# Attention scores as pairs of 64-row products, and the low parts of weight units on another engine

## The chip, the cores and the metric

The kernel runs on one core of one Trainium2 chip. The metric is the device time of one execution in microseconds, the median of several runs. The core has five engines that work from queues of their own: TensorE (PE; its weight loads are shown apart as PEld), VectorE (DVE), ScalarE (ACT), GpSimd (POOL), and SyncE (SP), which issues most of the transfers. Products are accumulated in PSUM; everything else lies in SBUF, both with 128 partitions.

## The reference

A small transformer of two layers works on 512 latent tokens with 256 context tokens ahead of them, 1024 features each. Layer 0 mixes the tokens with a bidirectional mLSTM, layer 1 with windowed attention; a squared-ReLU network follows each. The change lies in layer 1's attention alone:

```python
SWA_HEADS, SWA_KV_HEADS, SWA_DH = 16, 4, 64    # four query heads share one key head
# for each block j of 128 latent queries (four of them), each key head, its four query heads:
s_lat = where(valid, einsum("bqhgd,bkhd->bhgqk", qb, kb) * scale, -inf)  # blocks j-1, j, j+1
s_ctx = einsum("bqhgd,bchd->bhgqc", qb, ck) * scale                      # all 256 context tokens
m = max(max(s_lat), max(s_ctx), sink)
p = exp(s - m);  den = sum(p) + exp(sink - m)
o = (p_lat @ vb + p_ctx @ cv) / den
```

A key is valid for a query when they are at most 128 positions apart. The products must be more exact than one pass with the numbers' high parts, so each number is split: a high part that TensorE takes as it is, and a low part, the rest. A product of two split numbers is then high by high, high by low and low by high (low by low is small).

## The kernel before

The attention is worked in 16 tiles (g, j): key head g from 0 to 3, query block j from 0 to 3. The scores of a tile have 128 rows of queries for each of four heads, and W columns: the two or three neighbouring blocks of keys and 256 of context. W is 512 for j of 0 and 3, and 640 for j of 1 and 2.

**Queries and keys.** `q_out` (line 1888) turns the projected queries of one tile, splits them, and lays high and low part of a head side by side, 64 and 64 columns; a transpose puts them below one another, so that a head has 128 partitions: 64 of high part and 64 of low part. `kv_out` (line 1860) makes two copies of the keys in the same way: in k0 the high part lies above the low one, in k1 the low one above the high one. One 128-row product of a head with k0 gives high by high plus low by low, one with k1 gives the two mixed terms.

**Scores.** `scores` (line 1905) goes through the four heads one after the other. Each has two products for the 256 columns of context (lines 1927 and 1928) and two for the latent columns (1929 and 1934). Between the latter lie one or two products of a bf16 identity with a bf16 mask (1931, 1933) which add -1e30 where a key is out of the window: one for j of 0 and 3, two else. The result `s` is a PSUM tile of 1024 columns, which spans two banks; the pool `sc` has two buffers of it. A tile of 512 columns a head takes two heads into one buffer, one of 640 columns one head. When a buffer is full, VectorE takes the maximum (1940) and makes the negative bias nb (1942), and ScalarE makes the exponentials e with their sums (1947). For two heads at a time VectorE then makes the reciprocal of the denominator and GpSimd scales e (1958).

**Values.** `weigh` (line 1962) transposes the weights of a tile, 128 columns of all four heads at a time (1974), ScalarE takes the high part ph (1979) and VectorE the low part pl (1980), and two products with the values follow (1989, 1990).

**Order.** Everything is written as generators, and a pattern, `PAT` in line 18, says how the steps of a tile are interleaved: S is the next step of the scores of the tiles ahead, T a turn of weights, V a pair of value products, F a step of filler, that is of a projection of keys, values or queries for later tiles (six products of 256 columns) or of the output projection of the previous key head (three of 512 columns). Scores have four steps for each tile, one a head, and run somewhat more than a tile ahead. A scheduler then lays out each engine's instructions by readiness and priority; `keep_in_program_order` holds a single instruction behind its predecessor on the engine. On the chip each engine takes its instructions strictly in the order laid out.

**Weight units.** `unit` (line 73) loads 128 x 1024 weights by SyncE into `raw` (three buffers) and calls `split` (line 1034): ScalarE copies the high part `whi`, and the engine handed in, else VectorE, subtracts to get the low part `wlo` (line 1038). During the attention the units of the query projection (wsq, two for each key head) and of the output projection (wsout, two for each) come this way.

Layer 0 has 64-row products of its own, which the change doesn't touch: lines 931 and 988 take two heads of 64 features alternately, one in the upper and one in the lower 64 partitions, each into a PSUM bank of its own.

Of the kernel before, what the change touches and what calls it, by code (L numbers as in the profile page):

```python
# [9 lines left out]
F32 = mybir.dt.float32  # L10
F32R = mybir.dt.float32r
BF16 = mybir.dt.bfloat16
AF = mybir.ActivationFunctionType
ALU = mybir.AluOpType
# [7 lines left out]
P = 128  # L22
D = 1024
KT = D // P
NL = 512
NCX = 256
T = NL + NCX
# [7 lines left out]
DH = 64  # L35
# [21 lines left out]
class Trunk:  # L57
    def __init__(self, tc, ctx, aps):
        self.tc, self.nc, self.ctx, self.a = tc, tc.nc, ctx, aps
        self.nq = 0  # L60
        self.ada_todo = []
        self.ada_every = 0
        self.ada_cap = None
        self.pin = self.pin_mm = False
        self.ada_due = 0.0


# [966 lines left out]
    def split(self, src, hi, lo, eng=None):  # L1034

        keep = self.tc.keep_in_program_order if self.pin else lambda i: i
        keep(self.nc.scalar.copy(out=hi, in_=src))  # L1037
        keep((eng or self.nc.vector).tensor_tensor(out=lo, in0=src, in1=hi.bitcast(F32), op=ALU.subtract))  # L1038

    def feed(self, pin=False):  # L1040

# [590 lines left out]
    def layer1_mix(self, u):  # L1632
        nc, tc, a = self.nc, self.tc, self.a
        self.ctx_ada.close()
        with tc.tile_pool(name="sw", bufs=1, reuse_waits="tile") as sw:
# [8 lines left out]
            idb = sw.tile([P, P], BF16, name="idb")  # L1644
            nc.gpsimd.tensor_copy(out=idb, in_=self.ident)
            msk = []
# [37 lines left out]
            with tc.tile_pool(name="sc", bufs=2, space=PSUM, reuse_waits="tile") as sc, \  # L1684
# [33 lines left out]
                def filler(n):  # L1718
# [7 lines left out]
                        yield  # L1726
                    yield from its

                curs = [[] for _ in todo]

                def all_scores():
# [11 lines left out]
                for n, (g, j) in enumerate(todo):  # L1743
                    if ys[g] is None:
                        ys[g] = sw.tile([P, 2, NL], F32, name=f"yT{g}", tag="yT", bufs=2)
                    if j == 0 and g:
                        parts = self.out_part(g - 1, ys, pt, "pt")
                    if n == 14:
                        y3 = self.split_y(3)
                        st3 = {"y": y3}  # L1750
                        self.st = {}
                        self.tmpA = [self.base.tile([P, NL], F32, name=f"nA{t}", tag=t) for t in ("uH5", "uL5", "uL4")]
                        pa = self.out_part(3, ys, pt, "pt", "A", st3)
                        parts = [f for i in range(4) for f in (parts[i], pa[i])] + pa[4:5]
                        self.split_half(ys[3], y3, 0)
                    fl = filler(n)
                    wg = self.weigh(sw, g, j, curs[n], pt, av, ys)
                    for cmd in PAT if n < 15 else PL:
                        next({"S": sg, "F": fl}.get(cmd) or wg[cmd], None)
                    for it in (wg["T"], wg["V"], fl):  # L1760
                        for _ in it:
                            pass
# [97 lines left out]
    def kv_out(self, sw, pr, j, ps, eng):  # L1860

        nc = self.nc
        d = self.swd
        vt, v = d["vst"][j, pr], ps[:, 128:256].rearrange("p (h d) -> p h d", d=DH)
        nc.scalar.copy(out=vt[:, :, 0, :], in_=v)
        nc.vector.tensor_tensor(out=vt[:, :, 1, :], in0=v, in1=vt[:, :, 0, :].bitcast(F32), op=ALU.subtract)
        if j < 4:
            k = self.rope(sw, j, ps[:, 0:128], 2, eng)
        else:
            k = sw.tile([P, 640], F32, name="rp1", tag="e", bufs=12)[:, :128].rearrange("p (h d) -> p h d", d=DH)  # L1870
            nc.scalar.copy(out=k, in_=ps[:, 0:128].rearrange("p (h d) -> p h d", d=DH))

        sp = sw.tile([P, 2, 4, DH], F32R, name="ksp", tag="sp", bufs=4)
        kk = k.unsqueeze(2).broadcast_to([P, 2, 2, DH])
        nc.scalar.copy(out=sp[:, :, 0::3, :], in_=kk)
        nc.vector.tensor_tensor(out=sp[:, :, 1:3, :], in0=kk, in1=sp[:, :, 0::3, :].bitcast(F32), op=ALU.subtract)

        def late():
            pt = self.ptp.tile([P, 512], F32R, name="pt", tag=self.ptag)
            for i in range(2):  # L1880
                for h in range(2):
                    nc.tensor.transpose(out=pt[:, (2 * i + h) * P:(2 * i + h + 1) * P],
                                        in_=sp[:, h, 2 * i:2 * i + 2].rearrange("p a d -> p (a d)"), identity=self.identr)
            nc.any.tensor_copy(out=d["ks"][pr][:, :, :, j * P:(j + 1) * P],
                               in_=pt.rearrange("p (i h t) -> p i h t", i=2, h=2))
        return late

    def q_out(self, sw, g, j, ps, eng):
        nc = self.nc
        qs = self.swd["qs"]  # L1890
        q = self.rope(sw, j, ps, 4, eng)
        sp = sw.tile([P, 4, 2, DH], F32R, name="qsp", tag="sp", bufs=4)
        nc.scalar.copy(out=sp[:, :, 0, :], in_=q)
        nc.vector.tensor_tensor(out=sp[:, :, 1, :], in0=q, in1=sp[:, :, 0, :].bitcast(F32), op=ALU.subtract)

        def late():
            pt = self.ptp.tile([P, 512], F32R, name="pt", tag=self.ptag)
            for i in range(4):
                nc.tensor.transpose(out=pt[:, i * P:(i + 1) * P],
                                    in_=sp[:, i].rearrange("p a d -> p (a d)"), identity=self.identr)  # L1900
            qs[g, j] = sw.tile([P, 4, P], F32R, name="qs", tag="qs", bufs=5)
            nc.any.tensor_copy(out=qs[g, j], in_=pt.rearrange("p (h t) -> p h t", t=P))
        return late

    def scores(self, sw, g, j, scp, out):

        nc = self.nc
# [8 lines left out]
        nb = sw.tile([P, 4], F32, name="nb", tag="nb", bufs=2)  # L1916
        es = sw.tile([P, 4], F32, name="es", tag="es", bufs=2)
        per = 2 if W == 512 else 1
        views = []
        for i in range(4):  # L1920
            if i % per == 0:
                s = scp.tile([P, 1024], F32, name="s", tag="s")
                views = []
            ql = q4[:, i, :]
            c0 = (i % per) * 512 if per == 2 else 512 - wl
            lat, cx = s[:, c0:c0 + wl], s[:, c0 + wl:c0 + W]
            mm(out=cx, lhsT=ql, rhs=k0[:, NL:T], start=True, stop=False)
            mm(out=cx, lhsT=ql, rhs=k1[:, NL:T], start=False, stop=True)
            mm(out=lat, lhsT=ql, rhs=k0[:, lo * P:hi * P], start=True, stop=False)
            if j > 0:  # L1930
                mm(out=lat[:, 0:P], lhsT=d["idb"], rhs=d["msk"][0], start=False, stop=False)
            if j < 3:
                mm(out=lat[:, wl - P:wl], lhsT=d["idb"], rhs=d["msk"][1], start=False, stop=False)
            mm(out=lat, lhsT=ql, rhs=k1[:, lo * P:hi * P], start=False, stop=True)
            views.append(s[:, c0:c0 + W])
            if i % per == per - 1:
                i0 = i + 1 - per
                mx = sw.tile([P, 2], F32, name="mx", tag="mx", bufs=4)[:, 0:per]
                keep = self.tc.keep_in_program_order if g + j == 0 else lambda x: x
                keep(nc.vector.reduce_max(out=mx, in_=s.rearrange("p (h w) -> p h w", h=2) if per == 2 else views[0],  # L1940
                                          axis=AX.X))
                keep(nc.vector.scalar_tensor_tensor(
                    out=nb[:, i0:i0 + per], in0=mx, scalar=-(DH ** -0.5),
                    in1=d["nsink"][:, g * 4 + i0:g * 4 + i0 + per], op0=ALU.mult, op1=ALU.min))
                for ii, sv in zip(range(i0, i0 + per), views):
                    e = sw.tile([P, 640], F32, name="e", tag="e", bufs=12)
                    nc.scalar.activation(out=e[:, :W], in_=sv, func=AF.Exp, scale=DH ** -0.5, bias=nb[:, ii:ii + 1],
                                         accum_out=den[:, ii:ii + 1])
                    out.append(e)
            if i % 2:  # L1950
                pr = slice(i - 1, i + 1)
                nc.vector.tensor_tensor(out=es[:, pr], in0=nb[:, pr],
                                        in1=self.sink[:, g * 4 + i - 1:g * 4 + i + 1], op=ALU.add)
                nc.scalar.activation(out=es[:, pr], in_=es[:, pr], func=AF.Exp)
                nc.vector.tensor_tensor(out=den[:, pr], in0=den[:, pr], in1=es[:, pr], op=ALU.add)
                nc.vector.reciprocal(out=den[:, pr], in_=den[:, pr])  # L1956
                for ii in (i - 1, i):
                    nc.gpsimd.tensor_scalar(out=out[ii][:, :W], in0=out[ii][:, :W], scalar1=den[:, ii:ii + 1],  # L1958
                                            scalar2=1.0, op0=ALU.mult, op1=ALU.mult)
            yield  # L1960

    def weigh(self, sw, g, j, ps_, ptp, avp, ys):
# [194 lines left out]
```

## Time and profile before

| | |
|---|---|
| runs (three) | 1531.76, 1531.79, 1532.83 us, median 1531.79 |
| profiled execution | 1531.83 us |
| its span, first to last instruction | 1530.0 us |
| granted TensorE clock, mean | 0.997 |
| attention stage | about 955 to 1200 us of the span |
| score products (lines 1927 to 1934) | 352 matmuls, 955.8 to 1157.1 us |

In the profile's rows a line number stands for a line of the kernel, `out<-in` names tiles, and a shape such as 64*128 in a matmul's row gives the rows and columns of the array that it uses, followed by the shape that streams through. A group's row gives the time that the group kept its engine busy, the mean length of one instruction in ns, and, behind the second bar, how long the engine was idle ahead of them and what ended it. A row of a window gives its limits, its length, and for PE, PEld, DVE, ACT and POOL the busy time with the number of instructions, then the granted clock, the share of the transfers, and GB/s; asked for one tile, it leaves out engines that don't touch it. A row of the waits says who waited for whom, for how long in sum, how often, and the longest wait. Matmuls run in a pipeline: the length of one reaches beyond the start of the next.

### The profile page before, as it was taken

What the parts mean: (1) busy time and instruction counts of PE and PEld (TensorE: products, weight loads), DVE (VectorE), ACT (ScalarE), POOL (GpSimd) and SP (SyncE); (2) the same over time, 40 slices, a digit from 0 to 9 for tenths busy, and PEclk for the clock granted to TensorE, in tenths of its full rate; (3) what the DMA queues carried; (4) which work ended last, traced back from release to release, by engine and by line L of the source; (5) the groups of instructions that cost most, each with busy time, mean ns of one, the idle gap of its engine ahead of it and who ended that gap; (6) DMA issues with size and microseconds to landing.
All of it is one profiled execution on the core that took longest, in us unless ns stands there. A gap on an engine that the chain in (4) does not pass through costs nothing.

```text
span 1530.0 us, 23829 instructions
## 1 busy us (share of the span) xinstructions
PE 1505.8 (98%) x9129; PEld 1349.1 (88%) x9129; DVE 1135.0 (74%) x2074; ACT 739.8 (48%) x1494; POOL 310.7 (20%) x312
## 2 busy tenths in 40 slices
PE   9999999999999999999999999999999999999998
PEld 5888888878889999999999999888887988888886
DVE  4985638497797768777776668788888875757697
ACT  4544242443674352423515355575666665445454
POOL 0112021311203222322333230343443000000000
PEclk9999999999999999999999999999999999999999
DMA  9133313244132334244343422010101524140321
GB/s 378 70 102 120 111 56 121 66 148 148 56 97 69 124 125 151 97 152 131 131 152 103 145 73 73 29 42 28 56 31 39 182 94 138 55 152 28 110 70 55
DMA packets 46632, 157.27 MB, mean 103 GB/s; under 512 B 5135, under 2 KB 7695, under 8 KB 46391
## 3 DMA queue, kind: packets, MB, share of 16 engines
q1 hardware_dynamic: 45344, 154.25, 30.4%
q8 instruction: 72, 1.18, 0.3%
q10 hardware_dynamic: 1175, 1.51, 0.3%
q14 instruction: 41, 0.34, 0.1%
HBM read 153.64 MB, written 2.10 MB: 102 GB/s over the span
## 4 chain that ended last, share of the span: by engine, by line
PE 79%; DVE 7%; ACT 5%; issue 4%; POOL 3%; DMA 1%; POOLq 0%; DVEq 0%; ACTq 0%
PE mm L102 50%; PE p L102 7%; PE pj L102 4%; PE kept L102 3%; PE pt L1974 1%; PE acc L102 1%; PE pc L102 1%; PE at L993 1%; DVE adap L269 1%; ACT whi L1037 1%; DVE wlo L1038 1%; PE pb L102 1%; PE av L1989 1%; PE av L1990 1%; PE at L956 1%
## 5 line engine op out<-in xcount | busy, mean ns | idle before, releaser
L102 PE MATMUL mm<-h,whi 128*128 128x384 f32 x1024 | 264.1, 338 | 1.4 <-ACT h L1037 0.8
L1038 DVE TENSOR_TENSOR wlo<-raw,whi 128x1024 fp32r<-128x1024 f32 (+2 forms) x152 | 178.2, 1176 | 81.1 <-ACT whi L1037 78.9
L1037 ACT CAST whi<-raw 128x1024 fp32r<-128x1024 f32 (+2 forms) x152 | 150.8, 998 | 144.3 <-PE mm L102 96.1
L102 PE MATMUL mm<-uH,whi 128*128 128x512 f32 (+1 forms) x496 | 189.5, 386 | 0.0
L102 PEld LDWEIGHTS mm<-h,whi 128*128 128x128 f32 x1024 | 185.5, 188 | 4.1 <-ACT h L1037 1.9
L102 PE MATMUL mm<-uL,whi 128*128 128x512 f32 (+1 forms) x496 | 186.5, 378 | 0.8 <-DVE uL L339 0.4
L102 PE MATMUL mm<-uH,wlo 128*128 128x512 f32 (+1 forms) x496 | 186.9, 378 | 0.0
L269 DVE SCALAR_TENSOR_TENSOR adap<-raw,crow 128x1024 bf16<-128x1024 f32 x128 | 161.6, 1262 | 21.4 <-DMA raw<-ada 20.6
L102 PE MATMUL mm<-h,wlo 128*128 128x384 f32 x512 | 172.1, 336 | 0.0
L102 PE MATMUL p<-t,whi 128*128 128x384 f32 x448 | 114.2, 336 | 0.0
L1037 ACT CAST whi<-sum 128x512 fp32r<-128x512 f32 (+1 forms) x42 | 31.8, 760 | 159.8 <-PE mm L102 59.8
L102 PEld LDWEIGHTS mm<-uH,wlo 128*128 128x128 f32 x496 | 93.3, 188 | 17.8 <-issue 0.9
L102 PEld LDWEIGHTS mm<-uL,whi 128*128 128x128 f32 x496 | 93.6, 189 | 16.7 <-DVE uL L651 0.7
L102 PEld LDWEIGHTS mm<-uH,whi 128*128 128x128 f32 x496 | 92.9, 189 | 15.6 <-issue 0.3
L102 PEld LDWEIGHTS mm<-h,wlo 128*128 128x128 f32 x512 | 96.1, 188 | 0.0
L1038 DVE TENSOR_TENSOR wlo<-wb,whi 128x1024 fp32r<-128x1024 f32 x49 | 59.1, 1221 | 36.5 <-ACT whi L1037 36.3
L1038 DVE TENSOR_TENSOR h<-r,h 128x384 fp32r<-128x384 f32 (+2 forms) x100 | 58.5, 587 | 32.9 <-ACT h L1037 32.6
L102 PEld LDWEIGHTS p<-t,whi 128*128 128x128 f32 x448 | 81.3, 188 | 0.0
L102 PE MATMUL mm<-uC,whi 128*128 128x256 f32 x416 | 79.5, 290 | 0.3 <-ACT whi L1037 0.3
L1037 ACT CAST whi<-wb 128x1024 fp32r<-128x1024 f32 x49 | 51.5, 1054 | 57.5 <-PE mm L102 47.8
L102 PE MATMUL p<-t,wlo 128*128 128x384 f32 x224 | 75.3, 336 | 0.0
L1958 POOL TENSOR_SCALAR e<-e,den 128x512 f32<-128x512 f32 (+1 forms) x64 | 49.2, 783 | 126.9 <-DVE den L1956 80.2
(411 smaller groups left out, 3787.9 us busy)
## 6 DMA issues: line engine op xcount, KB each, us to landing
raw<-ada SPq DMA_DIRECT2D x80, 512.0 KB, 3.6
raw<-w SPq DMA_DIRECT2D x64, 512.0 KB, 3.5
raw<-w2a SPq DMA_DIRECT2D x32, 512.0 KB, 3.5
wb<-w2b SPq DMA_DIRECT2D x28, 512.0 KB, 4.1
adaw<-ada SPq DMA_DIRECT2D x16, 512.0 KB, 11.2
raw<-wqk SPq DMA_DIRECT2D x8, 512.0 KB, 4.0
raw<-wv SPq DMA_DIRECT2D x8, 512.0 KB, 3.5
raw<-wo SPq DMA_DIRECT2D x8, 512.0 KB, 3.5
```

Source lines behind the costliest of these rows:

```text
L102: i = self.nc.tensor.matmul(**kw)
L269: self.tc.keep_in_program_order(nc.vector.scalar_tensor_tensor(out=pr, in0=w, scalar=0.5, in1=self.crow[:, v, :], op0=ALU.mult, op1=ALU.mu ...
L956: mm(out=ps[64 * h:64 * h + 64, 0:VW], lhsT=kp[:, d, j, 64 * h:64 * h + 64], rhs=v[:, j, h, :], start=True, stop=True)
L993: mm(out=o[hh][:, i * VW:(i + 1) * VW], lhsT=pw[g, d, hh][:, i, :], rhs=v[:, 3 * g + i, hh, :], start=False, stop=i == 2)
L1037: keep(self.nc.scalar.copy(out=hi, in_=src))
L1038: keep((eng or self.nc.vector).tensor_tensor(out=lo, in0=src, in1=hi.bitcast(F32), op=ALU.subtract))
L1958: nc.gpsimd.tensor_scalar(out=out[ii][:, :W], in0=out[ii][:, :W], scalar1=den[:, ii:ii + 1], scalar2=1.0, op0=ALU.mult, op1=ALU.mult)
L1974: nc.tensor.transpose(out=pt[:, i * P:(i + 1) * P], in_=ps_[i][:, n * P:(n + 1) * P], identity=self.ident)
L1989: mm(out=o, lhsT=vv, rhs=ph, start=n == 0, stop=False)
L1990: mm(out=o, lhsT=vv, rhs=pl, start=False, stop=n == len(blks) - 1)
```

## The change

The scores of two heads are made together, and each product has 64 rows. The queries of two heads are laid so that after the transpose one tile has the high parts of both heads (the first in partitions 0 to 63, the second in 64 to 127) and another one their low parts. The keys are laid so that k0 has the high part twice, in the upper and in the lower half, and k1 the low part twice. There are three terms: high by k0, high by k1, low by k0. For each term the first head's product uses the upper 64 rows and the second head's the lower 64, one behind the other. First come the six products for the context columns, then the first term of the latent columns for both heads, then the masks of both heads (128 rows each, as before), then the two other terms. All of a pair's products but the first of the context part and the first of the latent part are kept in program order. For 640 columns a pair takes both buffers of `s` at once.

The scores still have four steps a tile: the first of a pair holds all its products and the first maximum with its exponentials (in a tile of 512 columns all of them), the second the rest.

Beside this, from the start of the attention until tile 14 of 0 to 15 is reached, `split` takes GpSimd for the low part where no engine is handed in.

```diff
@@ unit's low part
+        self.lo_eng = self.nc.vector
-        keep((eng or self.nc.vector).tensor_tensor(out=lo, in0=src, in1=hi.bitcast(F32), op=ALU.subtract))
+        keep((eng or self.lo_eng).tensor_tensor(out=lo, in0=src, in1=hi.bitcast(F32), op=ALU.subtract))
@@ layer1_mix
+                self.lo_eng = nc.gpsimd
                 curs = [[] for _ in todo]
...
                     if n == 14:
+                        self.lo_eng = nc.vector
@@ kv_out
-        nc.scalar.copy(out=sp[:, :, 0::3, :], in_=kk)
-        nc.vector.tensor_tensor(out=sp[:, :, 1:3, :], in0=kk, in1=sp[:, :, 0::3, :].bitcast(F32), op=ALU.subtract)
+        nc.scalar.copy(out=sp[:, :, 0:2, :], in_=kk)
+        nc.vector.tensor_tensor(out=sp[:, :, 2:4, :], in0=kk, in1=sp[:, :, 0:2, :].bitcast(F32), op=ALU.subtract)
@@ q_out
-        sp = sw.tile([P, 4, 2, DH], F32R, name="qsp", tag="sp", bufs=4)
+        sp = sw.tile([P, 2, 2, P], F32R, name="qsp", tag="sp", bufs=4)
+        q = q.rearrange("p (r h) d -> p r (h d)", r=2)
...
-                                    in_=sp[:, i].rearrange("p a d -> p (a d)"), identity=self.identr)
+                                    in_=sp[:, i // 2, i % 2], identity=self.identr)
@@ scores
+        def behind(n=1):
+            return self.tc.keep_in_program_order if n else lambda i: i
+        for pair in range(2):
+            ss = [scp.tile([P, 1024], F32, name="s", tag="s") for _ in range(2 // per)]
+            views = [ss[0][:, i * 512:i * 512 + W] if per == 2 else ss[i][:, c0:c0 + W] for i in range(2)]
+            rs = [slice(i * DH, (i + 1) * DH) for i in range(2)]
+            terms = [(q4[:, 2 * pair], k0), (q4[:, 2 * pair], k1), (q4[:, 2 * pair + 1], k0)]
+            for t, (ql, kp) in enumerate(terms):
+                for i in range(2):
+                    behind(t + i)(mm(out=views[i][:, wl:W], lhsT=ql[rs[i]], rhs=kp[rs[i], NL:T], start=t == 0, stop=t == 2))
+            for t, (ql, kp) in enumerate(terms):
+                for i in range(2):
+                    behind(t + i)(mm(out=views[i][:, :wl], lhsT=ql[rs[i]], rhs=kp[rs[i], lo * P:hi * P], start=t == 0,
+                                     stop=t == 2))
+                if t == 0:
+                    for lat in views:
+                        if j > 0:
+                            behind()(mm(out=lat[:, 0:P], lhsT=d["idb"], rhs=d["msk"][0], start=False, stop=False))
+                        if j < 3:
+                            behind()(mm(out=lat[:, wl - P:wl], lhsT=d["idb"], rhs=d["msk"][1], start=False, stop=False))
+            for n in range(2 // per):
...
+                if n == 0:
+                    yield
+            ...
             yield
```

The part of `scores` behind the products (maximum, bias, exponentials, denominator, scaling) has the same instructions as before.

More of the change, by code (lines that the diff above doesn't have):

```diff
@@ L1918, in scores @@
         per = 2 if W == 512 else 1
[L1919 to L1937, printed above, removed]
+        c0 = 0 if per == 2 else 512 - wl
@@ new lines, in behind @@
+        def behind(n=1):
[19 more added lines that the diff above has]
+            for n in range(2 // per):
+                i0 = 2 * pair + n * per
@@ L1938, in scores @@
                 mx = sw.tile([P, 2], F32, name="mx", tag="mx", bufs=4)[:, 0:per]
                 keep = self.tc.keep_in_program_order if g + j == 0 else lambda x: x
-                keep(nc.vector.reduce_max(out=mx, in_=s.rearrange("p (h w) -> p h w", h=2) if per == 2 else views[0],
+                keep(nc.vector.reduce_max(out=mx, in_=ss[0].rearrange("p (h w) -> p h w", h=2) if per == 2 else views[n],
                                           axis=AX.X))
@@ L1944, in scores @@
                     in1=d["nsink"][:, g * 4 + i0:g * 4 + i0 + per], op0=ALU.mult, op1=ALU.min))
-                for ii, sv in zip(range(i0, i0 + per), views):
+                for ii, sv in zip(range(i0, i0 + per), views[n * per:(n + 1) * per]):
                     e = sw.tile([P, 640], F32, name="e", tag="e", bufs=12)
@@ L1949, in scores @@
                     out.append(e)
[L1950 to L1959, printed above, removed]
+                if n == 0:
+                    yield
+            pr = slice(2 * pair, 2 * pair + 2)
+            nc.vector.tensor_tensor(out=es[:, pr], in0=nb[:, pr],
+                                    in1=self.sink[:, g * 4 + 2 * pair:g * 4 + 2 * pair + 2], op=ALU.add)
+            nc.scalar.activation(out=es[:, pr], in_=es[:, pr], func=AF.Exp)
+            nc.vector.tensor_tensor(out=den[:, pr], in0=den[:, pr], in1=es[:, pr], op=ALU.add)
+            nc.vector.reciprocal(out=den[:, pr], in_=den[:, pr])
+            for ii in (2 * pair, 2 * pair + 1):
+                nc.gpsimd.tensor_scalar(out=out[ii][:, :W], in0=out[ii][:, :W], scalar1=den[:, ii:ii + 1],
+                                        scalar2=1.0, op0=ALU.mult, op1=ALU.mult)
             yield
```

## The prediction

> **What bounds the kernel now.** I read the totals first, then the attention stage alone (955 to 1200 us, where the score products lie), then who waits there, then the chain of waits, then single instructions. The profiled execution took 1531.83 us, its span is 1530.0 us, and 1.83 us lie around the span; the median of the runs shown is 1531.79 us, 0.04 us away, so a difference worked out on the trace is added to the median as it is.
>
> The totals on the page; the engines in the stage; the score tile's own share of it:
>
> ```profile
> PE 1505.8 (98%) x9129; PEld 1349.1 (88%) x9129; DVE 1135.0 (74%) x2074; ACT 739.8 (48%) x1494; POOL 310.7 (20%) x312
> ...
> 955.00:1200.00 245.00, 235.64 (x1648) 206.53 (x1647) 201.22 (x439) 156.27 (x355) 93.19 (x123) 1.00 0.13 42
> ...
> 955.00:1200.00 245.00, 56.84 (x352) 40.01 (x256) 45.45 (x48) 51.19 (x128) 1.00 0.13 42
> ```
>
> In the stage PE is busy 235.64 of 245.00 us at a granted clock of 1.00, DVE 201.22, ACT 156.27, POOL 93.19. PE is idle for 9.36 us. Scores are 352 matmuls. Whatever PE is given in addition can hide only in those idle times. These are PE's two longest waits, and the chain of waits through the stage:
>
> ```profile
> PE s L1927 <- ACT e L1947: 2.9, 4, 1.2
> PE av L1990 <- DVE pl L1980: 1.0, 3, 0.6
> ...
> by line: PE mm L102 15.2%; PE pj L102 13.8%; PE pt L1974 8.9%; PE av L1989 6.3%; PE av L1990 5.6%; issue 4.1%; DVE pl L1980 3.5%; PE s L1934 3.3%; DVE mx L1940 3.1%; DVE wlo L1038 3.0%; ACT e L1947 2.5%; PE s L1927 2.4%; PE s L1929 2.3%; AC
> ```
>
> PE leads the chain; the low parts that are to move (DVE wlo) have 3.0% of it, 7.4 us.
>
> **The products themselves.** One head of a 640-wide tile, then one head of a 512-wide one, each up to the instruction behind it (start, length):
>
> ```profile
> 1018.79 0.28 PE L1927 MATMUL s<-ks,qs 128*128 128x256 f32 x1
> 1018.91 0.28 PE L1928 MATMUL s<-ks,qs 128*128 128x256 f32 x1
> 1019.03 0.34 PE L1929 MATMUL s<-ks,qs 128*128 128x384 f32 x1
> 1019.21 0.23 PE L1931 MATMUL s<-msk,idb 128*128 128x128 bf16 x1
> 1019.27 0.22 PE L1933 MATMUL s<-msk,idb 128*128 128x128 bf16 x1
> 1019.30 0.42 PE L1934 MATMUL s<-ks,qs 128*128 128x384 f32 x1
> 1019.56 0.60 PE L1974 MATMUL pt<-ident,e 128*128 128x128 f32 x4
> ...
> 1005.99 0.28 PE L1927 MATMUL s<-ks,qs 128*128 128x256 f32 x1
> ...
> 1006.59 0.60 PE L1974 MATMUL pt<-ident,e 128*128 128x128 f32 x4
> ```
>
> A head costs 0.77 us (1018.79 to 1019.56) or 0.60 us (1005.99 to 1006.59), so a pair of heads 1.54 or 1.20. Lengths overlap in these rows; the distance of two starts is the cost: 0.12 us for 256 columns, 0.18 for 384, 0.06 for a mask.
>
> Do two 64-row products run at once? Layer 0 has such pairs (L988), 129 columns each:
>
> ```profile
> 114.96 0.28 PE L102 MATMUL mm<-uC,wlo 128*128 128x256 f32 x1
> 115.17 0.94 PE L988 MATMUL at<-C,qs 64*128 64x129 f32 x12
> 116.04 1.05 PE L993 MATMUL at<-v,pw 128*128 128x129 f32 x7
> ...
> 223.28 0.28 PE L102 MATMUL mm<-whi,uC 128*128 128x256 f32 x1
> 223.49 0.72 PE L988 MATMUL at<-C,qs 64*128 64x129 f32 x8
> 224.13 1.27 PE L993 MATMUL at<-v,pw 128*128 128x129 f32 x9
> ```
>
> Twelve take 0.87 us until the next instruction, eight 0.64: four more, that is two pairs, cost 0.23, or 0.115 a pair. So they do, and a pair costs about what one product does. I take a pair's slot as 0.12 or 0.18 us. In three passes a pair of heads needs 3 x 0.12 + 3 x 0.18 + 4 x 0.06 = 1.14 us (before 1.54), or 6 x 0.12 + 2 x 0.06 = 0.84 (before 1.20). With 16 pairs of each width that is 16 x (0.40 + 0.36) = **-12.2 us**.
>
> **What the same rows charge for it.** The change of the array between 128-row and 64-row products has a price there. Eight products are four pairs, 0.46 us at 0.115, but take 0.64: 0.18 more. Before them a 256-column product lasts 0.21 us (223.28 to 223.49) instead of 0.12: 0.09 more. Behind them, nine L993 take 1.27 us; less the last one's own 0.27 that is 1.00 for eight steps, 0.125 each. The distance of undisturbed 129-column steps isn't in a row; taking the pair's 0.115 for it, 0.08 to 0.1 is extra. A visit to 64 rows costs about 0.37. I read this as four pieces of 0.09 to 0.1: at each of the two changes the old products run out, and then the first new weights are loaded in the open instead of under a running product.
>
> The change puts a 128-row mask product between the first and the second pass of the latent part, so each pair makes **two** visits: in, out to the masks, in again, out. That is four changes. The weights loaded at the change to the masks are bf16 and cheaper to load:
>
> ```profile
> L1934 PEld LDWEIGHTS s<-ks,qs 128*128 128x128 f32 x63 | 12.3, 195 | 0.0
> L1931 PEld LDWEIGHTS <-idb 128*128 128x128 bf16 x48 | 4.6, 96 | 3.9
> ```
>
> 96 ns against 195 halves that piece. Four run-outs of 0.09, three loads of 0.1 and one of 0.05 make 0.71 us a pair, and 32 pairs **+22.7 us**. No row shows a bf16 mask between two 64-row groups, so this is bounded: if the masks change nothing, one visit is left, 32 x 0.37 = 11.8 us; with all pieces full it is 32 x 0.76 = 24.3. I take 22.7, as the rows charge each change of shape that they show, whichever product stands beside it. By the Trainium skill (TensorEngine Tiling (Array Packing), Key Properties) a change of the tiling mode, and not of the tile alone, drains TensorE; the page gives no price. By that rule the masks, which use all 128 rows, count as a change each time, and the sum stays at the upper value.
>
> Products and changes together: -12.2 + 22.7 = **+10.5 us**, between -0.4 and +12.1.
>
> **The low parts.** Eleven units (two of wsq for each of three groups, two of wsout for groups 0 and 1, one for group 2 before the pointer goes back) leave VectorE for GpSimd.
>
> ```profile
> L1038 DVE TENSOR_TENSOR wlo<-raw,whi 128x1024 fp32r<-128x1024 f32 x18 | 22.5, 1253 | 0.5 <-ACT whi L1037 0.5
> ...
> L1857 POOL TENSOR_TENSOR rp<-rp,rp 128x256 f32<-128x256 f32 x14 | 10.3, 736 | 6.6 <-DVE rp L1856 3.4 <-PE av L1989 2.7
> ...
> L1146 POOL TENSOR_TENSOR sum<-raw 128x512 f32<-128x512 f32 x14 | 27.3, 1950 | 54.7 <-DVE t L1038 51.1 <-DVE wlo L1038 3.6
> ...
> L1147 POOL TENSOR_TENSOR sum<-raw,sum 128x512 f32<-128x512 f32 x14 | 19.0, 1356 | 1.1
> ```
>
> DVE is freed of 11 x 1.253 = 13.8 us. Of that the chain of waits can give back at most 7.4 x 11/18 = 4.5 us; PE's idle times name DVE seldom, so I take **-2**, between -4.5 and 0. GpSimd has no 1024-column subtraction in the trace: twice the 512-column rows is 2.7 to 3.9 us, so 30 to 43 us more on an engine that is busy 93 of 245. I count this at nothing: no idle time of PE in the stage is put down to a wlo, and GpSimd has 152 us free. If that cover is gone, a 3 us operation stands ahead of the rotary additions (L1857) and of the scaling of e on GpSimd's queue; ScalarE's copy of q waits for the former, and the exponentials stand behind that copy. I bound this by half of the eleven at one full length, 5 x 3 = 15 us, and zero.
>
> **The tile of scores.** In 640-wide tiles one head fills a buffer of the two, and now both are filled at once. The second pair must wait until both exponentials of the first are read; the product of its second head is held to program order, and transposes, values and fillers stand behind it on PE, for which ScalarE's ph and VectorE's pl wait.
>
> ```profile
> L1940 DVE TENSOR_REDUCE mx<-s 128x1 f32<-128x640 f32 x32 | 26.0, 815 | 2.0 <-PE s L1934 1.9
> L1942 DVE SCALAR_TENSOR_TENSOR nb<-mx,nsink 128x1 f32<-128x1 f32 x32 | 6.9, 217 | 0.1
> L1947 ACT ACTIVATE e<-s,nb 128x640 f32<-128x640 f32 x32 | 25.5, 799 | 12.8 <-DVE nb L1942 7.7 <-PE av L1990 3.9 <-DVE den L1956 0.8
> L1947 ACT ACTIVATION_READ_ACCUMULATOR e<-s,nb 128x1 f32 x64 | 12.8, 199 | 0.0
> L1980 DVE TENSOR_TENSOR pl<-pt,ph 128x512 fp32r<-128x512 f32 x72 | 48.9, 684 | 10.2 <-ACT ph L1979 9.0
> ```
>
> Two maxima and two nb are 2 x (0.815 + 0.217) = 2.06 us, the last exponential with its read 1.0: 3.1 us, and 4.4 with two pl between on VectorE. In the pattern T, F, T, F lie between the two pairs; two groups of transposes at about 0.4 and two fillers of six 0.12 products give 2.3 us. So 0.8 to 2.1 us are uncovered in each of eight tiles, 6 to 17 us, if nothing later moves up; five more items of the pattern may. I take **+2**, between 0 and 17. In 512-wide tiles a buffer holds both heads as before, and nothing is added. The new order of the split q and k has as many copies, subtractions and transposes as the old: nothing.
>
> Sum: 10.5 - 2 + 2 = +10.5; 1531.8 + 10.5 = **1542 us**.
>
> **Rivals.**
> (a) *The masks cost no change, or part of the changes falls into times when PE waits anyway.* One visit a pair: -12.2 + 11.8 - 2 + 2 = -0.4, about 1531. For it: no row shows the case, and PE idles 9.36 us. Against: 32 pairs make 64 visits, far more than PE has idle times.
> (b) *Changes cost nothing in this stream* (its products are twice to three times as long as those of L988 and may hide the loads): -12.2 - 2 + 2, about 1520, faster. Against it: the 256-column product ahead of L988 paid its 0.09 all the same.
> (c) *The score buffers or GpSimd's long operations stall PE*: 10.5 - 2 and 12 to 20 more, about 1556. It decides where the two uncovered microseconds of a 640-wide tile have no work to take their place.
> (d) *The halves don't overlap*, and the change doesn't do what it says: 12 slots in a row, 2.04 and 1.56 us, 16 x (0.50 + 0.36) = +13.8, with changes +36, about 1568. The 0.115 us a pair speaks against it.
> (e) *Each pass loads its weights in the open*: 32 x 6 x 0.1 = 19 us more, about 1561. At 0.115 a pair a load of 0.1 and a product can't stand one behind the other. The Trainium skill (TensorE: Matmul & The Clock Gate, The mechanism) has weight loads overlap running matmuls only where the row group differs; by that rule (e) comes out, and L988's repeated pairs, which use the same two row groups, disagree with it.
>
> **How the numbers follow.** Chances: the forecast 0.58, with a range of its own of 1536 to 1549; (a) 0.10; (b) 0.12; (c) 0.15; (d) and (e) 0.05. The range reaches down to (a) at 1530 and up to (c) at 1558 and leaves out (b), (d) and (e). A measurement of this kernel tells about 0.2%, 3.1 us, from no change. Faster by more: (b), 0.12. Within: most of (a), 0.08. Slower: the rest, 0.80.
>
> **What would show it.** Rows of s with 64*128 whose starts lie under 0.02 us apart in twos (against d); the distance from the first pair of a visit to the second about 0.1 longer than that of later pairs, and the last product ahead of the masks 0.09 longer than its columns (against a and b); 64-row groups falling into two parts for each pair; PE's time for a pair of heads about 1.85 and 1.55 us; the stage's length up by some 10 us with PE idle about as before. PE waiting for e or qs by more than 10 us in sum would make it (c). A stage shorter than 245 us would prove the prediction wrong at the price of the changes.

## The result: 1557.3 us, slower by 1.66%

The changed kernel takes 1557.34 us (median of four runs, 1556.77 to 1557.75), the kernel before 1531.78 us (four runs). The ratio is 1.0166, with an interval of 1.0149 to 1.0184: +25.6 us, where +10.5 was forecast.

The page of the changed kernel begins with its span and the totals of the engines:

```profile
span 1555.4 us, 24076 instructions
## 1 busy us (share of the span) xinstructions
PE 1522.5 (98%) x9256; PEld 1349.3 (87%) x9257; DVE 1138.4 (73%) x2066; ACT 738.9 (48%) x1491; POOL 335.7 (22%) x323
```

The span is longer by 25.4 us. PE is busy for 1522.5 - 1505.8 = 16.7 us more, and idle for 32.9 us instead of 24.2 (span less busy time), 8.7 more. So this isn't only more work on PE.

All of it lies in the attention stage. The first score product starts at 955.9 us as before; the last product with the values lies at 1199.8 us instead of 1174.5. The stage as a whole, and a part of it (window, its length, then PE, PEld, DVE, ACT and POOL with their counts, the granted clock, the share of the transfers, GB/s):

```profile
955.00:1225.00 270.00, 251.90 (x1774) 206.29 (x1774) 203.43 (x431) 155.22 (x352) 118.25 (x134) 0.97 0.12 38
...
1000.00:1050.00 50.00, 44.96 (x310) 37.09 (x307) 33.56 (x70) 27.41 (x62) 22.41 (x25) 0.90 0.10 32
```

PE is idle for 18.1 us of the stage (before 9.4), and the granted clock, 1.00 through the stage before, is 0.97, in these 50 us 0.90. The waits of PE in this stage (who waited for whom: sum, times, longest):

```profile
PE pt L1987 <- DVE qs L1908: 5.6, 3, 2.9
PE pt L1987 <- DVE hL L1835: 2.8, 3, 1.6
PE pt L1987 <- DVE rp L1860: 2.5, 2, 2.4
PE s L1937 <- ACT e L1959: 1.8, 2, 1.3
```

Before, the longest wait was 1.2 us and was for ScalarE's exponentials. That wait has shrunk from 2.9 to 1.8 us in sum, and VectorE is now the releaser of the long ones.

**One such wait.** The order of time around 1018 us, all engines (start, length, engine, line; in brackets the idle time ahead and who ended it):

```profile
1017.61 2.36 POOL L1039 TENSOR_TENSOR wlo<-raw,whi 128x1024 fp32r<-128x1024 f32 x1 [2.57 <-ACT whi L1038]
...
1017.86 2.13 DVE L1954 SCALAR_TENSOR_TENSOR nb<-mx,nsink 128x2 f32<-128x2 f32 x1
...
1020.02 0.16 DVE L1965 TENSOR_TENSOR es<-nb,sm 128x2 f32<-128x2 f32 x1
...
1020.10 0.68 DVE L1908 CAST qs<-pt 128x512 fp32r<-128x512 f32 x1
...
1020.84 1.11 PE L1987 MATMUL pt<-ident,e 128*128 128x128 f32 x4 [2.19 <-DVE qs L1908]
...
1021.88 1.01 PE L1937 MATMUL s<-ks,qs 64*128 64x256 f32 x6
```

The negative bias nb, two columns, takes 2.13 us on VectorE (its median is 0.16). It ends at 1019.99, when GpSimd's low part ends (1017.61 + 2.36 = 1019.97). The cast of qs, which empties a transpose tile, stands behind it, and PE idles 2.19 us for that tile. Then PE is slow: four transposes take 1.11 us and not 0.60, six products 1.01 and not 0.63. Windows of five microseconds show why:

```profile
1015.00:1020.00 5.00, 3.65 (x28) 3.05 (x26) 4.38 (x4) 1.94 (x3) 2.40 (x2) 1.00 0.00 0
1020.00:1025.00 5.00, 4.16 (x21) 2.87 (x22) 2.65 (x7) 2.60 (x7) 1.36 (x2) 0.55 0.32 105
1025.00:1030.00 5.00, 5.00 (x32) 4.57 (x32) 1.69 (x6) 2.89 (x8) 0.29 (x1) 0.76 0.00 0
```

The granted clock is 0.55 and 0.76 in the ten microseconds behind the wait: (0.45 + 0.24) x 5 makes at most 3.5 us more, an estimate.

**The score products.** A pair of heads of a 640-wide tile in the changed kernel, PE alone:

```profile
1052.47 0.63 PE L1937 MATMUL s<-ks,qs 64*128 64x256 f32 x6
1052.93 0.34 PE L1940 MATMUL s<-ks,qs 64*128 64x384 f32 x2
1053.21 0.23 PE L1945 MATMUL s<-msk,idb 128*128 128x128 bf16 x1
...
1053.54 0.62 PE L1940 MATMUL s<-ks,qs 64*128 64x384 f32 x4
1054.09 0.39 PE L103 MATMUL pj<-whi,uH 128*128 128x256 f32 x1
1054.31 0.28 PE L103 MATMUL pj<-wlo,uH 128*128 128x256 f32 x1
```

Six context products take 0.46 us: three pairs at 0.115 and 0.11 more. A latent pair takes 0.28 until the masks: 0.18 and 0.10 more. Four masks take 0.33: 0.24 and 0.09 more. Two pairs take 0.55: 0.36 and 0.19 more. The product behind takes 0.22 instead of 0.12. With the run-out of the product ahead (0.09) the changes of shape cost 0.68 us, and the pair of heads 0.09 + 1.62 + 0.10 = 1.81 us, 1.54 before. The 512-wide pair shows 1.32 us between first product and next instruction, 1.51 with entry and exit (1.20 before).

The trace has something else besides, in nine of the sixteen 640-wide pairs. In the changed kernel at 1032 us:

```profile
1032.07 0.28 PE L103 MATMUL pj<-whi,uL 128*128 128x256 f32 x1
1032.28 0.38 PE L1937 MATMUL s<-ks,qs 64*128 64x256 f32 x1
1032.59 0.38 PE L103 MATMUL pj<-whi,uH 128*128 128x256 f32 x1
1032.81 0.28 PE L103 MATMUL pj<-wlo,uH 128*128 128x256 f32 x1
```

The first head's first product stands alone. In a 640-wide pair the second head goes into the second buffer. The likely reason is that this one isn't free yet, so that the scheduler lays other work between the two; no 512-wide pair of this kernel is split, but no run tries it. The array changes to 64 rows and back for one product. It costs 0.31 us until the next instruction, 0.09 ahead and 0.10 behind, 0.50 in all. Nothing of it is saved later: the fifteen products left of such a pair take 1.60 us, as all sixteen of an unsplit one do.

### The profile page after: what moved, and what is told of

The parts are those of the page before. It is cut to its first block, busy times and chain, and to the rows that moved or that the text cites. A ratio compares the mean times of both kernels' runs of the same rounds, so it can differ in the third digit from the quotient of the medians.

```text
span 1555.4 us, 24076 instructions
## 1 busy us (share of the span) xinstructions
PE 1522.5 (98%) x9256; PEld 1349.3 (87%) x9257; DVE 1138.4 (73%) x2066; ACT 738.9 (48%) x1491; POOL 335.7 (22%) x323
## 3 DMA queue, kind: packets, MB, share of 16 engines
q10 hardware_dynamic: 1175, 1.51, 0.3%
## 4 chain that ended last, share of the span: by engine, by line
PE 67%; DVE 11%; ACT 7%; POOL 7%; issue 5%; DMA 2%; POOLq 0%; DVEq 0%; ACTq 0%
PE mm L103 44%; PE pj L103 3%; PE p L103 3%; DVE adap L270 3%; PE kept L103 2%; ACT whi L1038 2%; PE pt L1987 1%; PE acc L103 1%; DVE wlo L1039 1%; PE at L994 1%; POOL r L1239 1%; DMA raw<-w 1%; PE s L1940 1%; ACT r L1234 1%; DMA raw<-ada 1%
## 5 line engine op out<-in xcount | busy, mean ns | idle before, releaser
L1039 DVE TENSOR_TENSOR wlo<-raw,whi 128x1024 fp32r<-128x1024 f32 (+2 forms) x141 | 164.0, 1168 | 79.6 <-ACT whi L1038 77.2
```

Of the source, the lines that this page charges most:

```text
L1039: keep((eng or self.lo_eng).tensor_tensor(out=lo, in0=src, in1=hi.bitcast(F32), op=ALU.subtract))
```

## The experiments

**Theories.** Either the two halves of the change add up, the pairs with the +10 of the forecast and GpSimd's low parts with the other 15; or the pairs cost it all, through the score buffers. If the low parts cost, there are again two ways: the reading (VectorE's instructions are held while GpSimd reads SBUF) or the queue (GpSimd's long operations make late what stands behind them on GpSimd).

**1. The pairs alone.** As after, but every low part stays on VectorE.

```diff
-                self.lo_eng = nc.gpsimd
+                self.lo_eng = nc.vector
```

> The change without its GpSimd part: all low parts stay on VectorE. Theory: two causes add up, about 12 to 15 us from the score pairs (four changes of the array's shape a pair, and first products that stand alone), and about 10 to 13 us from GpSimd's low parts of 2.4 us, behind which VectorE's instructions with two SBUF inputs stand until PE is idle and its clock falls. Then this kernel takes 1542 to 1547 us, the granted clock is 1.00 in every 50 us of the stage, and no wait of PE is over 1.5 us. Rival 1: the score pairs alone make all of it (two buffers filled at once): 1553 to 1558 us.

Measured: 1542.72 us, ratio 1.0066 (1.0051 to 1.0081), +10.4 us. The page of this run:

```profile
span 1541.8 us, 24086 instructions
...
PE 1518.1 (98%) x9256; PEld 1346.6 (87%) x9257; DVE 1140.0 (74%) x2075; ACT 739.4 (48%) x1493; POOL 312.3 (20%) x312
```

PE is busy 12.3 us more than before, and idle 23.7 us, 0.5 less. The visits explain 16 x (0.31 + 0.27) = 9.3 us and the nine lone products of this run 9 x 0.50 = 4.5, 13.8 in all, against +11.8 in this span and +10.4 in the median. So the sum gives the size and not the last microseconds; three further splits of pairs, and the clock, aren't in it. The clock wasn't at 1.00 throughout, as expected, but at 0.96 between 955 and 1000 us. The score buffers don't carry the loss: PE's longest wait for an exponential is 0.6 us.

**2. The low parts alone.** The kernel before, with line 1038 and the switch of engine from the change and nothing else.

```diff
+                self.lo_eng = nc.gpsimd
...
                     if n == 14:
+                        self.lo_eng = nc.vector
```

> The kernel before with the GpSimd part alone: 11 low parts on GpSimd, the scores as before. Theory of two causes: VectorE's nb, es or qsp lengthened to about 2 us behind a low part, several times, and a time of 1536 to 1546 us. Rival 1 (the score pairs make all of it): 1530 to 1533 us.

Measured: 1546.32 us, 1.0087 (1.0072 to 1.0102), +14.0 us. 10.4 + 14.0 = 24.4 of the 25.6: the halves add up. Its page:

```profile
span 1544.7 us, 23820 instructions
...
PE 1511.4 (98%) x9128; PEld 1353.0 (88%) x9129; DVE 1142.3 (74%) x2066; ACT 739.7 (48%) x1491; POOL 335.2 (22%) x323
```

The same matmuls as before are busy 5.6 us longer; the granted clock, 0.98 from 955 to 1200 us and 1.00 before, explains about 5 of them. PE idles 33.3 us, 9.1 more. DVE lost eleven subtractions of 1.25 us and yet is busy 7.3 us longer. One place of its order of time says why; the row of nb gives counts and shortest/median/longest ns, and the second fence is of the kernel before:

```profile
979.67 2.38 POOL L1039 TENSOR_TENSOR wlo<-raw,whi 128x1024 fp32r<-128x1024 f32 x1
...
980.10 1.97 DVE L1945 SCALAR_TENSOR_TENSOR nb<-mx,nsink 128x1 f32<-128x1 f32 x1
...
L1945 DVE SCALAR_TENSOR_TENSOR nb<-mx,nsink x48: 132/160/2286, 959.1 to 1175.4; 128x1 f32<-128x1 f32 x32, 128x2 f32<-128x2 f32 x16
```

```profile
L1942 DVE SCALAR_TENSOR_TENSOR nb<-mx,nsink x48: 139/153/646, 958.6 to 1160.7; 128x1 f32<-128x1 f32 x32, 128x2 f32<-128x2 f32 x16
```

This is the rule and not an accident: eleven instructions with two operands from SBUF began on VectorE with more than 0.1 us of a low part ahead of them, and ten of them lasted until it ended. The other one began in its first 0.01 us.

**3. The same subtraction, needed by nobody.** The kernel before; VectorE still makes every low part, and GpSimd makes eleven of them once more into a tile that nothing reads.

```diff
+        if self.more and not eng and len(src.shape) == 2 and src.shape[-1] == D:
+            self.nc.gpsimd.tensor_tensor(out=self.spare, in0=src, in1=hi.bitcast(F32), op=ALU.subtract)
```

> The kernel before, all low parts on VectorE, and beside them an unused subtraction of the same kind on GpSimd for each of the 11 units (two SBUF inputs, 1024 columns). Theory: a GpSimd instruction of 2.4 us that reads SBUF holds VectorE's instructions with two SBUF inputs, whoever needs its result; nb, es, den or qsp lengthened to about 2 us as in the kernel with the low parts alone, and 1544 to 1556 us. Rival 4 (the low parts come too late for TensorE, or whi is read too late): nothing waits for the result here, so 1531 to 1534 us.

Measured: 1554.11 us, 1.0145 (1.0130 to 1.0160), +22.2 us. No instruction waits for the result, so it isn't a result that comes late from GpSimd that costs; nor is any wait of PE in run 2 or in the changed kernel put down to a low part. But this run costs more than run 2, and one reason can be read: VectorE's own low parts run into the copies, and three take 2.5 to 3.4 us instead of 1.2.

**4. GpSimd as long, but reading nothing.** The same place, a fill of 2560 columns.

```diff
+            self.tc.keep_in_program_order(self.nc.gpsimd.memset(self.spare, 0.0))
```

> The same, but the unused GpSimd instruction is a fill with zeros of 2560 columns, about 2.4 us, which reads nothing from SBUF. Theory (the reading of SBUF by both engines is what excludes): VectorE's instructions keep their lengths and the time is 1531 to 1536 us. Rival 5 (GpSimd's queue: the scaling of e and the rotary additions come late behind a long instruction): the same time as with the unused subtraction, 1544 to 1556 us.

Measured: 1534.01 us, 1.0013 (1.0003 to 1.0022), +2.1 us. GpSimd's added instruction and nb in run 3, then in run 4:

```profile
L1041 POOL TENSOR_TENSOR spare<-raw,whi x11: 2339/2387/3372, 979.8 to 1126.8; 128x1024 f32<-128x1024 f32 x11
...
L1948 DVE SCALAR_TENSOR_TENSOR nb<-mx,nsink x48: 133/156/2318, 959.3 to 1185.1; 128x1 f32<-128x1 f32 x32, 128x2 f32<-128x2 f32 x16
```

```profile
L1041 POOL MEMSET spare<- x11: 2232/2237/2241, 991.5 to 1145.9; 128x2560 f32 x11
...
L1948 DVE SCALAR_TENSOR_TENSOR nb<-mx,nsink x48: 141/154/678, 959.3 to 1163.4; 128x1 f32<-128x1 f32 x32, 128x2 f32<-128x2 f32 x16
```

Eleven instructions of nearly the same length on the same queue; with the reading one nb reaches 2318 ns, with the fill 678, near the 646 of before. The fills lie 2 to 27 us later in the stage than the subtractions, but they weren't out of VectorE's way: nineteen of its instructions with two operands from SBUF began under a fill, and none was more than 0.01 us longer than usual. So the long instruction on the queue explains some 2 us, and the reading the rest.

**5. Two of the held instructions freed, before and after.** nb takes its second operand as a scalar for each partition, and the sink's exponential is made by ScalarE with a bias instead of VectorE's addition es; the arithmetic is the same. In the kernel before, and in the changed one:

```diff
-                keep(nc.vector.scalar_tensor_tensor(out=nb[..], in0=mx, scalar=-(DH ** -0.5), in1=d["nsink"][..], ...))
+                for c in range(per):
+                    keep(nc.vector.tensor_scalar(out=nb[..], in0=mx[:, c:c + 1], scalar1=-(DH ** -0.5), scalar2=d["nsink"][..], ...))
...
-                nc.vector.tensor_tensor(out=es[:, pr], in0=nb[:, pr], in1=self.sink[..], op=ALU.add)
-                nc.scalar.activation(out=es[:, pr], in_=es[:, pr], func=AF.Exp)
+                    nc.scalar.activation(out=es[:, c:c + 1], in_=nb[:, c:c + 1], func=AF.Exp, bias=self.sink[..])
```

> The kernel before with two small steps written with one SBUF input: nb as a tensor_scalar with the sink as a per-partition scalar, one instruction a head, and es not by an addition on VectorE but as ScalarE's exponential of nb with the sink as bias. The sums are the same. Theory: nb is no longer held behind the scaling of e (up to 0.65 us in the kernel before), all its instances stay under 0.25 us, and the time is 1526 to 1532 us. Rival 6 (a VectorE instruction with any SBUF input is held): nb still reaches 0.5 us, 1531 to 1535 us.

> The whole change with nb and es written with one SBUF input as in the kernel ahead; the low parts stay on GpSimd. Theory: of the instructions that were held for 2 us, nb and es are free and qsp, y and den are not, so about half of the 14 us comes back: 1545 to 1551 us. Rival 6: 1555 to 1559 us.

Measured: 1532.13 us (1.0002, 0.9992 to 1.0011) from before, and 1552.00 us (1.0132, 1.0117 to 1.0147) from after. In the first, nb with one tensor operand is never held, though it is 50 ns longer:

```profile
L1943 DVE TENSOR_SCALAR nb<-mx,nsink x64: 193/206/216, 958.5 to 1160.7; 128x1 f32<-128x1 f32 x64
```

So freeing these two gains the kernel before nothing measurable, and in the changed one it gives back 5.3 of the 15 us, a little less than was expected. ksp and qsp (the low parts of keys and queries), y and den, which also take two operands from SBUF, are still held there: the longest of each took 2.13, 0.88, 1.22 and 1.09 us.

**6. The low part in quarters.** As after, each low part on GpSimd as four subtractions of 256 columns.

```diff
+        c = n // 4 if e is self.nc.gpsimd and len(src.shape) == 2 and n == D else n
+        for o in range(0, n, c):
```

> The whole change, but each low part on GpSimd as four subtractions of 256 columns (about 0.74 us each, 3.0 in sum instead of 2.4). Theory of two causes: it is the length of a single GpSimd instruction that holds VectorE and lets PE's clock fall; no VectorE instruction is longer than by about 0.75 us, the granted clock stays at 1.00, and the time is 1542 to 1549 us. Rival 2: it is the amount of work on GpSimd, or its queue, that counts: 1556 to 1562 us, since that amount grows.

Measured: 1550.62 us, 1.0122 (1.0105 to 1.0139): 6.7 us better than after, but between the two ranges expected. GpSimd and VectorE in this run:

```profile
1087.70 4.87 POOL L1043 TENSOR_TENSOR wlo<-raw,whi 128x256 fp32r<-128x256 f32 x7
...
1089.44 1.09 DVE L1958 SCALAR_TENSOR_TENSOR nb<-mx,nsink 128x1 f32<-128x1 f32 x2
...
1090.56 0.65 DVE L1969 TENSOR_TENSOR es<-nb,sm 128x2 f32<-128x2 f32 x1
```

The quarters follow each other without a pause, so nb, nb and es are each held by another one: a hold is no longer 2.3 us, but one comes after the other.

**7. One visit a pair.** As run 1, with the masks behind all three latent terms.

```diff
-                if t == 0:
-                    for lat in views:
+            for lat in views:
...
```

> The pairs without the GpSimd part as in the first kernel, but the masks come behind all three latent terms, so that a pair visits the 64-row shape once and not twice; the products are the same. Theory: a visit costs about 0.37 us, so 32 fewer visits give back 9 to 13 us: 1531 to 1537 us. Rival 3: the masks between the terms cost no change of shape of their own, and the price lies in waits for the score buffers: within 2 us of the first kernel of this call.

Measured: 1538.66 us, 1.0040 (1.0025 to 1.0055), 4.1 us better than run 1: less than the theory's 9 to 13, more than the rival's 2. The order of time on PE:

```profile
1003.22 0.63 PE L1937 MATMUL s<-ks,qs 64*128 64x256 f32 x6
1003.69 0.51 PE L1940 MATMUL s<-ks,qs 64*128 64x256 f32 x6
1004.13 0.29 PE L1946 MATMUL s<-msk,idb 128*128 128x128 bf16 x2
1004.23 0.48 PE L2001 MATMUL av<-ph,vst 128*128 128x512 f32 x1
```

The visit takes 1.01 us and not 1.32, and a 640-wide one 1.28 and not 1.60, so the masks' place costs 0.32 us a pair, 10 us in 32. PE's busy time does fall by 8.6. The page:

```profile
span 1538.3 us, 24085 instructions
...
PE 1509.5 (98%) x9256; PEld 1343.9 (87%) x9257; DVE 1139.3 (74%) x2073; ACT 740.6 (48%) x1495; POOL 313.2 (20%) x312
```

PE is idle for 28.8 us, 5.1 more than in run 1: about half of the gain became waiting.

**8. One visit, with the freed instructions of run 5.** Were those 5 us VectorE held behind GpSimd's short instructions?

> The kernel with one visit a pair and all low parts on VectorE, and nb and es written with one SBUF input. Open is why one visit gave back 4 us and not 10. If VectorE's instructions held behind GpSimd's short ones (scaling, rotary additions, 0.7 us) made the rest, this kernel comes to 1532 to 1535 us. If it is the order of the work instead (both score buffers filled at once, a lone first product, waits for pl and for the copy of qs), the time stays at 1537 to 1540 us with PE's waits as they were.

Measured: 1542.32 us, 1.0064 (1.0052 to 1.0076), no faster than run 7 and above both ranges. So they weren't. PE's first waits in the stage:

```profile
PE av L2003 <- DVE pl L1993: 3.0, 5, 1.2
PE s L1937 <- ACT e L1959: 2.2, 2, 1.6
```

What keeps the rest of run 7's gain stays open; the candidates are both score buffers filled at once, the lone products, and the order that the scheduler lays out, which differs in each of these kernels. No version was faster than the kernel before. Masks as 64-row halves weren't tried.

## Why the prediction was right or wrong

- **The price of the pairs: right.** Products and changes were put at +10.5 us, and with the 2 for the score buffers at +12.5; the pairs alone measure +10.4. By rows: 1.81 and 1.51 us a pair (forecast 1.85 and 1.55), 0.68 us of changes (forecast 0.71). The pair's slot of 0.115 and 0.18 us, and the masks as a full change, are as forecast; rival (a) in its first form, no change at the masks, is refuted by the 0.32 us of run 7, and (b), (d) and (e) by the same rows. Part of the agreement is luck: the sum of the visits is 9.3, and 4.5 of lone products, which the forecast didn't have, are nearly balanced by 3.4 that don't show in the median (0.5 of it is idle time of PE that was filled; the rest isn't accounted for).
- **The score buffers: mis-sized, and small.** +2, between 0 and 17, was taken for waits. In the changed kernel PE's wait for e is 1.8 us in sum, less than before. What they seem to cost instead is the lone products, 4.5 us by the sum above.
- **The low parts: this step failed.** It said "-2, between -4.5 and 0", and of GpSimd "I count this at nothing: ... GpSimd has 152 us free". Measured: +14.0 alone. GpSimd's instruction takes 2.4 us, a little below the estimated 2.7 to 3.9, and there was indeed room in its queue. But free time of an engine was the wrong measure: while it reads, VectorE's instructions with two operands from SBUF stand still. The other half of the term, the time that VectorE is freed of, can't be read alone: run 3 with VectorE's own low parts costs 22.2 us and run 2 without them 14.0, but in run 3 these collide with the copies.
- **Rival (c)** gave 1556 us with a chance of 0.15, and its number is nearly the result. Half of its mechanism holds: GpSimd's long operations stall PE. But its way was GpSimd's queue, and run 4 shows that the queue is worth 2 us; and the other half, the score buffers, isn't there. The sign set for it, PE waiting for e or qs by more than 10 us in sum, isn't met either: 1.8 + 5.6 + 0.7 = 8.1.
- **The sign to look for** was in the trace of before. VectorE's nb had a mean of 217 ns in the quoted group, and its row by counts, shown with run 2, has a median of 153 and a longest of 646 ns. What held it could be read as well. The longest one, at 969.93, and the scaling of e on GpSimd both end at 970.58:

```profile
969.00 1.58 POOL L1958 TENSOR_SCALAR e<-e,den 128x640 f32<-128x640 f32 x2 [2.36 <-DVE den L1956]
...
969.93 0.65 DVE L1942 SCALAR_TENSOR_TENSOR nb<-mx,nsink 128x1 f32<-128x1 f32 x1
```

- **PE idle "about as before"** held for run 1 (23.7 against 24.2 us), not for the whole change (32.9).

What isn't settled is the size of the loss. If the length of each VectorE instruction beyond the lower quartile of its own form is summed over the stage (those over 0.15 us), it is 7.5 us before, 24.0 in run 2 and 13.6 in the changed kernel; yet the low parts cost 14.0 in the one and 14.6 in the other (1557.3 - 1542.7). So the sum of the holds doesn't give the price. Where a hold falls, whom it makes late and whether the clock drops behind it are likely to decide; no run parts these.

## What to carry to other kernels

Before work is moved to an idle engine, ask what else it will stop: look in the trace for short VectorE instructions with two SBUF operands whose longest is a multiple of their median, and see whether they end with GpSimd's. An engine's free time is no estimate of what it can take over; an unused copy of the moved work, as in run 3, shows in one run whether it disturbs, though not by how much (22.2 us there, 14.0 for the move itself). And where products of two array shapes alternate, count the changes (here 0.16 us each) as well as the products.

## What the runs showed of the hardware

**GpSimd and VectorE exclude each other.** An instruction of VectorE that takes two operands from SBUF is held until a reading GpSimd instruction ends: nb took 2.13 us instead of 0.16, es 2.20. One that reads PSUM isn't: the maxima, casts and pl that began under a low part in the changed kernel were at most 0.02 us longer than usual. In the changed kernel, VectorE's order of time and then GpSimd's:

```profile
1095.52 1.55 DVE L1952 TENSOR_REDUCE mx<-s 128x1 f32<-128x640 f32 x2
1096.98 0.74 DVE L1954 SCALAR_TENSOR_TENSOR nb<-mx,nsink 128x1 f32<-128x1 f32 x2
1097.76 2.20 DVE L1965 TENSOR_TENSOR es<-nb,sm 128x2 f32<-128x2 f32 x1
```

```profile
1095.25 4.69 POOL L1039 TENSOR_TENSOR wlo<-raw,whi 128x1024 fp32r<-128x1024 f32 x2
```

The two maxima take their usual 0.8 us each under GpSimd's first low part, nb waits for its end, and es ends with the second one at 1099.95. The Trainium skill (SBUF — State Buffer, Who interferes with whom) states this: the two engines share a pair of ports, the one that starts first holds it for its whole instruction, and a VectorE instruction with two SBUF inputs contends with a GpSimd instruction that reads SBUF, not with one that only writes. Runs 2 to 4 agree (nb up to 2286 and 2318 ns under reading instructions, 678 with the fill), and so does a GpSimd subtraction of run 3 that took 3372 ns instead of 2387 when a low part on VectorE had begun 0.10 us ahead of it. The prediction should have used it.

**The clock can fall after short idle times.** The wait of 2.19 us at 1018.65 was followed by a granted clock of 0.55 and 0.76 over ten microseconds. The Trainium skill (TensorE: Matmul & The Clock Gate, Part 1) has the clock fall after an idle window of about 3.4 us; by that rule this wait was too short, and the trace disagrees. Not every such wait does it: one of 2.15 us in run 3, from 1049.32 us on, was followed by 1.00, while in run 1 the clock was 0.70 from 965 to 970 us with no wait over 0.7 us since the stage began. What decides isn't shown.

**A change of the array's shape costs about 0.16 us.** Run 7 saves two changes a pair and 0.32 us with them, though the products in between are only bf16 masks of 0.06 us each; the four changes of a pair in the rows of the result make 0.68, 0.17 each.
